# GpSimd makes the lower part of every second half block of split weights

## The chip, the cores and the metric

The kernel runs on one core of one Trainium2 chip. The metric is the device time of one execution in microseconds (us). Before the change three runs took 1807.63 us in the median, from 1806.89 to 1811.34.

## What is computed

The reference passes a 256 x 1024 activation through three blocks, all in float32: a block of chunkwise retention and a gated linear recurrence, a block of windowed attention, convolution and pooling with a convolutional feed-forward network, and a block of two layers, each of a SwiGLU network, a mixer (an RWKV-7 time mix in the first layer, a chunked gMLP in the second), cross-attention to a memory, and a second SwiGLU network.

```python
def reference(x, ...):
    x = first_block(x, ...)    # q,k,v,g,x_lru,g_lru = split(norm(x) @ w_in); retention, RG-LRU; h + mixed @ w_out
    x = second_block(x, ...)   # h = x @ w_in; attention, conv, pool; layer norms; (u * silu(g)) @ w_down
    return third_block(x, ...) # per layer: ffn1, mixer, cross-attention, ffn2, each x + f(rms_norm(x)) @ w
```

Nearly all of the work is products of the 256 rows with weight matrices of 1024 to 5632 columns. Every weight is used once.

## The kernel before, in words

All weights lie in device memory as blocks of 128 x 2048 floats (`WB = 2048`), in the order in which they are used (the plan). For accuracy a product is made from three matmuls: a float32 weight w is split into an upper part hi (w rounded to the matmul's type `fp32r`) and a lower part lo = w - hi; the activations are split likewise, and the product is hi·hi + hi·lo + lo·hi (`mul`, lines 533 to 547, and `mul_tok`, lines 549 to 567; line 547, 563 and 566 are those that read a block's lower part). Only the blocks of three matrices (`WHOLE`: rw_k, rw_v, rw_o) are used unsplit. Each of the four SwiGLU networks takes 33 blocks (22 + 11).

A block goes through these steps, each into one of 21 slots of on-chip memory (SBUF):

- `_dma` (line 429): SyncE (SP) issues the load of one raw block into a free slot.
- `_split` (line 444): makes half a block. It takes a slot for hi and lo of this half, issues the copy that rounds hi on ScalarE (ACT, line 455), and leaves the subtraction that makes lo on VectorE (DVE, line 458) in `self.rest`. The subtraction is issued by the next call of `_rest`. After that of the second half (`part` is 1) the raw block's slot is given back.
- `pump` (line 478): called after every eight or so groups of matmuls. It issues loads while there are slots to spare, then one `_split`, up to `SPLIT = 4` blocks ahead of the block in use, and else `_rest`.
- `take` and `second` (lines 498 and 518): hand a block to the matmuls. `_need` (line 509) first makes whatever half is not yet made.

There is no scheduler behind this: each engine executes its instructions in the order in which the program issues them. VectorE's queue holds, beside the 524 subtractions of line 458, nearly all elementwise work of the mixers, the norms and the evictions from the matmul's accumulators (PSUM). GpSimd (POOL) has 33 small instructions: memsets, eight copies of four columns (line 1819, `pend`), and one masking of the gMLP's 128 x 2048 mixing weights (`affine_select`, line 1557).

Of the kernel before, what the change touches and what calls it, by code (L numbers as in the profile page):

```python
# [10 lines left out]
F32 = mybir.dt.float32  # L11
# [290 lines left out]
class Net:  # L302
# [138 lines left out]
        self.queue = max(self.queue, self.clock + self.LAT) + us  # L441
        return self.queue

    def _split(self):

        i, part = self.split_i, self.part
        t = self.slot([P, 2, WB // 2], R32)
        if part == 0:
            self.hl[i] = Block()
        self.hl[i].parts.append(t)  # L450
        s = slice(part * WB // 2, (part + 1) * WB // 2)
        hi, lo = t[:, 0], t[:, 1]
        raw = self.raw[i]
        self._rest()
        self.nc.scalar.copy(hi, raw[:, s])  # L455

        def rest():
            self.nc.vector.tensor_sub(lo, raw[:, s], hi.bitcast(F32))  # L458
            if part:
                self.drop(self.raw.pop(i))  # L460
        self.rest, self.rest_of = rest, (i, part)
        self.part = 1 - part
        self.split_i += part

    def _whole(self):

# [42 lines left out]
    def _need(self, i, part):  # L509
        while (self.split_i, self.part) <= (i, part):  # L510
            if self.dma_i <= i:
                self._dma()
            if not self._whole():
                self._split()
        if self.rest and self.rest_of <= (i, 1):
            self._rest()

# [1773 lines left out]
```

## Time and profile before

| what | value |
|---|---|
| median of three runs | 1807.63 us |
| the profiled execution, its own time | 1807.12 us |
| its span (first to last instruction) | 1805.4 us |
| TensorE matmul busy (PE) | 1776.4 us |
| VectorE busy (DVE) | 1256.9 us |
| ScalarE busy (ACT) | 914.0 us |
| GpSimd busy (POOL) | 13.4 us |

The time around the span is 1.7 us. PE is the matmul engine, PEld its weight loads, which overlap the matmuls. A busy share is an average over stages with different limits; what a stage is bound by is read from the windows, the waits and the chain of that stage. Names such as s, t, psd and psx are the program's tiles: s and t lie in SBUF, psd and psx in PSUM. L458 is line 458.

### The profile page before, as it was taken

How to read it: one execution, taken by the hardware profiler on the slowest of the kernel's cores; microseconds unless marked ns; L12 is line 12 of the kernel's file. 1: busy time of each engine (PE TensorE's matmuls, PEld its weight loads, DVE VectorE, ACT ScalarE, POOL GpSimd, SP SyncE). 2: the span in 40 equal slices, each digit the busy share in tenths (PEclk: the TensorE clock that was granted, in tenths of full speed). 3: DMA queues.
4: the chain of work that ended last, by engine and by line, in shares of the span. 5: the costliest groups of instructions: out<-in, count | busy, mean ns of one | idle time of the engine just before them, and what ended most of it. 6: DMA issues, size and time to landing. Idle time of an engine off the chain costs nothing.

```text
span 1805.4 us, 27651 instructions
## 1 busy us (share of the span) xinstructions
PE 1776.4 (98%) x11142; PEld 1552.9 (86%) x11142; DVE 1256.9 (70%) x2300; ACT 914.0 (51%) x1550; POOL 13.4 (1%) x33
## 2 busy tenths in 40 slices
PE   9999999999999999999999999999999999999997
PEld 8899889899887888888698888888888899888886
DVE  7897878997757646678777765566556588675553
ACT  7778455665536544072225554444444455454451
POOL 0000000000000000001000000000000000000000
PEclk9999999999999999999899999999999999999999
DMA  8445435454553645603433454455445636345450
GB/s 317 148 184 207 172 140 214 163 186 162 210 210 140 210 163 187 238 24 117 141 118 118 186 187 163 169 216 198 164 163 190 254 117 229 145 169 182 163 187 24
DMA packets 55495, 310.34 MB, mean 172 GB/s; under 512 B 13727, under 2 KB 16840, under 8 KB 19144
## 3 DMA queue, kind: packets, MB, share of 16 engines
q1 hardware_dynamic: 55368, 308.59, 47.0%
q8 instruction: 87, 1.43, 0.3%
q14 instruction: 40, 0.33, 0.1%
HBM read 304.36 MB, written 4.21 MB: 171 GB/s over the span
## 4 chain that ended last, share of the span: by engine, by line
PE 89%; DVE 7%; ACT 2%; issue 1%; DMA 1%; SPq 0%; DVEq 0%; ACTq 0%
PE psd L543 17%; PE psd L547 14%; PE psd L562 10%; PE psd L564 10%; PE psd L563 10%; PE psd L545 5%; PE psd L546 5%; DVE s L458 2%; PE psx L543 2%; PE psd L2169 2%; PE psd L557 1%; PE psd L540 1%; PE psx L1451 1%; PE psx L547 1%; ACT s L366 1%
## 5 line engine op out<-in xcount | busy, mean ns | idle before, releaser
L458 DVE TENSOR_TENSOR s<-s,s 128x1024 fp32r<-128x1024 f32 x524 | 627.1, 1221 | 169.8 <-ACT s L455 169.4
L547 PE MATMUL psd<-s,s 128*128 128x256 f32 x2336 | 656.8, 281 | 3.0 <-DVE s L458 2.8
L455 ACT CAST s<-s 128x1024 fp32r<-128x1024 f32 x524 | 532.2, 1046 | 179.9 <-PE psd L547 99.8
L543 PE MATMUL psd<-s,s 128*128 128x512 f32 x1392 | 492.7, 398 | 0.9 <-DVE s L629 0.9
L547 PEld LDWEIGHTS psd<-s,s 128*128 128x128 f32 x2336 | 443.1, 190 | 4.7 <-DVE s L458 4.2
L562 PE MATMUL psd<-s,s 128*128 128x512 f32 x816 | 323.8, 397 | 0.7 <-ACT s L366 0.7
L564 PE MATMUL psd<-s,s 128*128 128x512 f32 x816 | 318.6, 390 | 0.7 <-DVE s L369 0.7
L563 PE MATMUL psd<-s,s 128*128 128x512 f32 x816 | 317.8, 389 | 0.0
L543 PEld LDWEIGHTS psd<-s,s 128*128 128x128 f32 x1392 | 261.4, 188 | 64.0 <-DVE s L629 1.3
L545 PE MATMUL psd<-s,s 128*128 128x256 f32 x944 | 271.7, 288 | 0.0
L546 PE MATMUL psd<-s,s 128*128 128x256 f32 x944 | 266.9, 283 | 0.0
L564 PEld LDWEIGHTS psd<-s,s 128*128 128x128 f32 x816 | 153.1, 188 | 34.1 <-DVE s L369 1.3
L545 PEld LDWEIGHTS psd<-s,s 128*128 128x128 f32 x944 | 180.8, 192 | 1.6 <-DVE s L458 0.6
L546 PEld LDWEIGHTS psd<-s,s 128*128 128x128 f32 x944 | 180.9, 192 | 0.1
L562 PEld LDWEIGHTS psd<-s,s 128*128 128x128 f32 x816 | 153.3, 188 | 31.6 <-ACT s L366 1.0
L563 PEld LDWEIGHTS psd<-s,s 128*128 128x128 f32 x816 | 153.4, 188 | 30.5
L1455 DVE TENSOR_TENSOR s<-psx,s 128x512 fp32r<-128x512 f32 x44 | 30.4, 692 | 94.7 <-ACT s L1457 79.2
L366 ACT ACTIVATE t<-psd,rc 128x256 f32<-128x256 f32 x88 | 41.5, 475 | 99.1 <-PE psd L564 96.5
L1457 ACT CAST s<-psx 128x512 fp32r<-128x512 f32 x40 | 23.5, 587 | 120.7 <-PE psx L1451 120.7
L369 DVE SCALAR_TENSOR_TENSOR t<-psd,rc,t 128x256 f32<-128x256 f32 x88 | 41.5, 482 | 47.5 <-ACT t L366 47.5
L366 ACT ACTIVATE t<-x 128x256 f32<-128x256 f32 x86 | 34.2, 407 | 69.1 <-DVE x L369 45.2
L366 ACT ACTIVATE s<-x,vecs 128x256 fp32r<-128x256 f32 (+1 forms) x80 | 40.2, 505 | 49.5 <-DVE x L1415 36.3
(382 smaller groups left out, 1848.8 us busy)
## 6 DMA issues: line engine op xcount, KB each, us to landing
s<-w_ffn_in SPq DMA_DIRECT2D x88, 1024.0 KB, 4.8
s<-w_ffn_out SPq DMA_DIRECT2D x44, 1024.0 KB, 4.8
s<-w_up SPq DMA_DIRECT2D x22, 1024.0 KB, 4.8
s<-w_out SPq DMA_DIRECT2D x12, 1024.0 KB, 5.0
s<-w_down SPq DMA_DIRECT2D x11, 1024.0 KB, 4.8
s<-w_xq SPq DMA_DIRECT2D x8, 1024.0 KB, 5.8
s<-w_xo SPq DMA_DIRECT2D x8, 1024.0 KB, 5.2
s<-w_gm_v SPq DMA_DIRECT2D x8, 1024.0 KB, 4.8
```

What stands on the lines that cost most here:

```text
L366: return self.nc.scalar.activation(out, in_, func, **kw)
L369: return self.nc.vector.scalar_tensor_tensor(out, in0, scalar, in1, op0=op0, op1=op1)
L455: self.nc.scalar.copy(hi, raw[:, s])
L458: self.nc.vector.tensor_sub(lo, raw[:, s], hi.bitcast(F32))
L543: mm(out, w[0], x.two(k), start=first, stop=False)
L545: mm(out[:, :T], w[0], x.hi(k), start=first, stop=False)
L546: mm(out[:, :T], w[0], x.lo(k), start=False, stop=False)
L547: mm(out[:, :T], w[1], x.hi(k), start=False, stop=last)
L562: mm(out, hi, w[0], start=first, stop=False)
L563: mm(out, hi, w[1], start=False, stop=False)
L564: mm(out, lo, w[0], start=False, stop=last)
L2169: mm(ps[:, :P], blocks[m // 2][j * P:(j + 1) * P][0], yo[:, k, o], start=k == 0, stop=k == KD - 1)
```

## The change

The subtraction of every second half of a block is issued to GpSimd instead of VectorE, directly behind the copy on ScalarE and not at the next `_rest`, and the raw block's slot is given back there. First halves stay on VectorE. A second half that `_need` makes because the matmuls want it at once (`now=True`) stays on VectorE as before.

```diff
-    def _split(self):
+    def _split(self, now=False):
         i, part = self.split_i, self.part
         t = self.slot([P, 2, WB // 2], R32)
...
         self._rest()
         self.nc.scalar.copy(hi, raw[:, s])
+        self.part = 1 - part
+        self.split_i += part
+        if part and not now:
+            self.nc.gpsimd.tensor_sub(lo, raw[:, s], hi.bitcast(F32))
+            self.drop(self.raw.pop(i))
+            return
 
         def rest():
             self.nc.vector.tensor_sub(lo, raw[:, s], hi.bitcast(F32))
             if part:
                 self.drop(self.raw.pop(i))
         self.rest, self.rest_of = rest, (i, part)
-        self.part = 1 - part
-        self.split_i += part
...
             if not self._whole():
-                self._split()
+                self._split(now=True)
```

## Rows read from the trace of the kernel before

**Rows 1.** The page's first part: busy us, share of the span, instructions.

```profile
PE 1776.4 (98%) x11142; PEld 1552.9 (86%) x11142; DVE 1256.9 (70%) x2300; ACT 914.0 (51%) x1550; POOL 13.4 (1%) x33
```

**Rows 2.** Waits: who waited for whom, us in total, times, longest.

```profile
PE psd L547 <- DVE s L458: 2.8, 4, 1.6
...
PE psx L1089 <- DVE acc L1079: 0.8, 1, 0.8
...
PE psd L543 <- DVE s L629: 0.9, 1, 0.9
...
SPq L434 <- DVE s L458: 489.0, 85, 23.2
```

**Rows 3.** Groups by line: busy us, mean ns | idle before, releaser.

```profile
L458 DVE TENSOR_TENSOR s<-s,s 128x1024 fp32r<-128x1024 f32 x524 | 627.1, 1221 | 169.8 <-ACT s L455 169.4
```

**Rows 4.** Timeline, GpSimd's copies beside VectorE: start, us, engine, what.

```profile
806.64 1.02 POOL L1819 COPY pend<-e 128x4 f32<-128x4 f32 x1
...
812.69 0.19 POOL L1819 COPY pend<-e 128x4 f32<-128x4 f32 x1 [0.42 <-ACT e L366]
...
806.40 1.22 DVE L458 TENSOR_TENSOR s<-s,s 128x1024 fp32r<-128x1024 f32 x1
```

**Rows 5.** Timeline, VectorE beside GpSimd's masking, and the same operation elsewhere.

```profile
1406.44 2.01 POOL L1557 TENSOR_SCALAR_AFFINE_SELECT s<-s 128x2048 f32<-128x2048 f32 x1 [554.24 <-DMA s<-ws]
...
1406.80 1.67 DVE L374 TENSOR_SCALAR rc<-rcv 128x2 int32<-128x2 int32 x1
...
559.72 0.17 DVE L374 TENSOR_SCALAR rc<-rcv 128x2 int32<-128x2 int32 x1
```

**Rows 6.** Windows: length, busy us (count) of PE, PEld, DVE, ACT, POOL; clock, DMA, GB/s.

```profile
25.00:50.00 25.00, 24.88 (x143) 22.11 (x144) 24.40 (x48) 20.42 (x38) 0.00 (x0) 1.00 0.70 272
...
75.00:100.00 25.00, 24.78 (x201) 23.80 (x201) 24.14 (x46) 18.09 (x30) 0.00 (x0) 1.00 0.44 152
100.00:125.00 25.00, 25.00 (x203) 24.60 (x202) 24.66 (x54) 15.85 (x38) 0.00 (x0) 1.00 0.44 165
...
1100.00:1125.00 25.00, 25.00 (x117) 20.75 (x116) 13.61 (x16) 12.27 (x16) 0.00 (x0) 1.00 0.44 160
...
1450.00:1475.00 25.00, 23.36 (x197) 23.16 (x196) 23.83 (x40) 14.59 (x24) 0.00 (x0) 1.00 0.36 127
```

**Rows 7.** Groups by line on VectorE between 25 and 50 us.

```profile
L369 DVE SCALAR_TENSOR_TENSOR s<-s,vecs,s 128x253 f32<-128x253 f32 (+2 forms) x24 | 11.3, 481 | 0.6
L458 DVE TENSOR_TENSOR s<-s,s 128x1024 fp32r<-128x1024 f32 x7 | 8.4, 1218 | 0.0
```

**Rows 8.** The same between 75 and 125 us.

```profile
L458 DVE TENSOR_TENSOR s<-s,s 128x1024 fp32r<-128x1024 f32 x17 | 20.4, 1217 | 0.5 <-ACT s L455 0.5
```

**Rows 9.** The same between 350 and 400 us.

```profile
L458 DVE TENSOR_TENSOR s<-s,s 128x1024 fp32r<-128x1024 f32 x22 | 26.7, 1218 | 1.6 <-ACT s L455 1.6
L369 DVE SCALAR_TENSOR_TENSOR t<-psd,vecs,t 128x255 f32<-128x255 f32 (+1 forms) x38 | 18.1, 479 | 0.7
```

**Rows 10.** The same between 1450 and 1475 us.

```profile
L458 DVE TENSOR_TENSOR s<-s,s 128x1024 fp32r<-128x1024 f32 x11 | 13.2, 1216 | 0.0
```

**Rows 11.** The chain that ended last, 300 to 335 us: start, us, what.

```profile
316.46 2.35 DVE s L458 x2
...
325.09 3.49 DVE s L458 x3
```

**Rows 12.** Timeline of ScalarE's copies at four tight places, and one subtraction.

```profile
20.87 1.03 ACT L455 CAST s<-s 128x1024 fp32r<-128x1024 f32 x1
...
63.46 1.03 ACT L455 CAST s<-s 128x1024 fp32r<-128x1024 f32 x1
...
64.53 1.23 DVE L458 TENSOR_TENSOR s<-s,s 128x1024 fp32r<-128x1024 f32 x1 [1.87 <-ACT s L455]
...
555.05 3.88 ACT L455 CAST s<-s 128x1024 fp32r<-128x1024 f32 x4
...
1447.34 1.98 ACT L455 CAST s<-s 128x1024 fp32r<-128x1024 f32 x2
```

## The prediction, as it was put on record before the result was known

> **What bounds the kernel now.** I read the page's engine line first. TensorE is busy 1776.4 us of the span of 1805.4 [rows 1], so all that any change off TensorE can give back is 1805.4 - 1776.4 = 29.0 us, the start and the end of the program among them. VectorE at 1256.9 us is not the bound on average. The waits come next: TensorE waited for a subtraction of line 458 four times, 2.8 us together and 1.6 the longest, and about 0.8 or 0.9 us for each of two other VectorE results [rows 2]. So nearly everywhere the split weights lie ready before they are wanted. The windows say where that is less sure: in a long feed-forward stage VectorE is busy 13.61 of 25 us with TensorE at 25.00, but in the first block it is busy 24.40, 24.14 and 24.66 of 25, and in the gMLP 23.83 [rows 6]. There VectorE has no time left, and whatever it loses it can't make up in that stage.
>
> **What is removed.** 524 subtractions at 1221 ns [rows 3], half of them second halves: 262. With four waits on line 458 in all [rows 2] few can be urgent ones, so I count 262 moved. On VectorE each costs 1.17 us, since two in a row take 2.35 [rows 11]: 262 x 1.17 = 307 us less on an engine that is not the bound. This by itself is worth only what TensorE waits for.
>
> **What is added.** 262 two-input operations of 128 x 1024 on GpSimd. The trace has none. The nearest row is the masking, 2048 elements read once in 2.01 us [rows 5]. From below: 1024 elements at that rate, 1.0 us, if both inputs come at once. From above I allow 4.0 us, twice that row. I take 2.0 us: two inputs of 1024 are as many elements read as in that row. 262 x 2.0 = 524 us on GpSimd, which has 13.4 us of other work [rows 1], so GpSimd itself has room.
>
> By the Trainium skill (GPSIMD Engine Reference, Performance versus the Vector engine) an addition of 2048 float32 elements takes GpSimd 4497 ns, two inputs sharing one read port. Half of that would be an estimate of 2.25 us; the sum below would grow by 3.9 us. No run here shows it yet.
>
> **The two engines exclude each other.** This is what the price hangs on. A GpSimd copy of four columns takes 0.19 us at 812.69, but 1.02 us at 806.64, and then it ends at 807.66, just as the VectorE subtraction that began at 806.40 and took 1.22 us ends [rows 4]. The other way round, a VectorE operation on two columns, 0.17 us at 559.72, took 1.67 us at 1406.80 and ended at 1408.47, with the masking on GpSimd that ran from 1406.44 to 1408.45 [rows 5]. So each 2.0 us on GpSimd may close VectorE for 2.0 us to instructions that read two tiles in SBUF (s<-s,s), while 1.17 us are saved: a loss of up to 0.83 us of VectorE time for each half moved. Instructions that read PSUM and one SBUF tile (t<-psd,vecs,t) I take to go on.
>
> The Trainium skill says the same of such instructions (SBUF — State Buffer, Who interferes with whom): an exclusive lock, one side waits for the whole of the other's instruction. The two pairs of rows agree; that it holds for a two-input VectorE operation behind a GpSimd subtraction no row here shows.
>
> **The sum, stage by stage.** Where VectorE has slack (13.61 of 25 us [rows 6]) the exchange costs nothing: the first lower parts are wanted long after they are made. That cover would go only if GpSimd took about 4 us (a rival below). In the full stages:
> - 25 to 50 us: 7 subtractions [rows 7], 3.5 moved: -3.5 x 1.17 = -4.1. Blocked: 3.5 x 2.0 x the share of two-tile instructions in what stays. Line 369 there is s<-s,vecs,s, 11.3 us, and with half of line 458's 8.4 that is 15.5 of the 20.2 left, 0.77; other small groups have the same form, so I take 0.9: +6.3. Net +2.2, of which the 0.6 us of idle time [rows 6] takes some: 1.6 us late. TensorE waits for line 458 in this part, so I count it whole.
> - 75 to 125 us: 17 subtractions [rows 8], 8.5 moved: -9.9; blocked at the same share 8.5 x 2.0 x 0.9 = +15.3; idle 0.86 + 0.34 [rows 6]: 4.2 us late. TensorE is at 24.78 and 25.00, so the weights are some way ahead; I count half, 2.1.
> - 350 to 400 us: 22 subtractions [rows 9], 11 moved: -12.9. Line 369 there reads PSUM, 18.1 us that are not blocked, beside 13.4 us of line 458 that stays; with small groups the blocked share is about 0.54: +11.9. Nothing.
> - 1450 to 1475 us: 11 subtractions [rows 10], 5.5 moved: -6.4; share about 0.8: +8.8; idle 1.2 [rows 6]: +1.2.
> Then single places, where a second half falls into a chain that TensorE waits for. The copy that began at 20.87 ends at 21.9, GpSimd holds until 23.9 and a chain of tiny VectorE operations (a reciprocal root) stands still: 2.0 less the 1.17 saved, +0.8. The copy of 63.46 ends at 64.5; the lower part is ready at 66.5 and not at 65.76 (64.53 + 1.23): +0.7. At 555.05 four copies in a row give GpSimd two subtractions ahead of another such chain: +0.8. At 1447.34 two copies, the first one a second half: GpSimd runs from about 1448.3 to 1450.3, over the chain that ends in the wait of 1.6 us for line 458: +2.0 [rows 2, 12].
> Gains: between 300 and 335 us VectorE is the chain, with pairs of subtractions (2.35) and a run of three (3.49) [rows 11]. Half of them leave, and TensorE's two waits there, 0.8 (L1089) and 0.9 (L629) [rows 2], go: -1.7. What is late next is TensorE itself, whose matmuls stand in a fixed order, so the 4 us and more that VectorE gains there give no more.
> Sum: 1.6 + 2.1 + 0 + 1.2 + 0.8 + 0.7 + 0.8 + 2.0 - 1.7 = +7.5 us.
>
> **Moved steps.** The raw block's slot is given back one pump earlier, so SP is told of the next load earlier, but it then waits for GpSimd instead of VectorE. SP waits for line 458 now, 489.0 us in 85 waits up to 23.2 [rows 2], and TensorE doesn't notice; lower parts that end up to 0.83 us later, or some us earlier where they stood behind other VectorE work, change nothing. It costs something only where weights are scarce, which are the stages counted above. Behind a waiting GpSimd subtraction stand GpSimd's own 33 instructions, most of them memsets far from any split; the eight copies of line 1819 lie in a stage with four split blocks, and I cost them at nothing (one late by 2.0 us would cost at most that).
>
> The profiled execution took 1807.12 us: 1807.1 + 7.5 = 1814.6. The median of the runs lies 0.5 above it: **1815.1 us**.
>
> **The rivals.**
> *Faster: VectorE's relief reaches TensorE.* The second halves no longer stand in VectorE's queue in front of evictions and norms, and GpSimd begins right behind the copy. It needs the short subtraction: below 1.17 us GpSimd blocks VectorE for less than it saves, so that is the point from which it decides. For it speaks that VectorE is the chain from 300 to 335 us [rows 11]; against it the two pairs of rows on exclusion. The three waits of rows 2 make 4.5 us; with as much again hidden in delayed evictions, a quarter of the 29.0 us: -7, 1800.6.
> *No change.* GpSimd falls into VectorE's gaps, the losses of single places are 0.8 here and there and the gains 1.7; it also is the result if most halves turn out urgent and stay on VectorE, so that the change doesn't do what it says. For it: TensorE at 25.00 in most windows. 1807 to 1809.
> *Far slower: GpSimd takes 4 us.* In the feed-forward window TensorE runs 117 matmuls [rows 6], 24 a block (four steps, two halves of the rows, three matmuls): 4.9 blocks, one in 5.1 us. GpSimd would close 4.9 x 4.0 = 19.6 us, and of VectorE's 13.61 us 13.61 - 4.9 x 1.17 = 7.9 stay: 27.5 us do not fit into 25, 10% too much. The four SwiGLU networks have 132 blocks, 670 us; since part of the 7.9 us reads PSUM I take half of 10%: +34, 1841. It decides from about (25 - 7.9) / 4.9 = 3.5 us.
>
> **How the numbers follow.** A change within 0.3%, 5.4 us, is what a measurement of this kernel can't tell from none. The forecast (slower, 1813.1 to 1823, its own range, the upper end from 2.25 us a subtraction and the 75 to 125 us term counted whole) has 0.41; far slower 0.07; no change 0.30; faster 0.22. So slower 0.48, same 0.30, faster 0.22. The range holds 8 in 10 from 1800 (most of the faster case) to 1836 (about 2.7 us a subtraction in the full stages); the far end of the last rival is left out.
>
> **What would show it.** Right: GpSimd has about 262 subtractions; VectorE operations of 0.17 or 0.42 us that last 1 to 2 us beside them; TensorE waits for VectorE that grow before 130 us and near 1450 us; feed-forward windows unchanged at 25.00. Wrong: two-tile VectorE operations of ordinary length beside a GpSimd subtraction (then the exclusion is not there and the faster rival stands), a subtraction far from 2.0 us, or a loss that sits in stages where VectorE had slack.

## The result, and the profile after

The changed kernel takes 1832.53 us in the median (1830.45 to 1833.55), the kernel before 1808.97 in the same comparison: ratio 1.0126, 95% interval 1.0113 to 1.0139. Slower was forecast, and 1832.5 lies inside the range, but the forecast loss was 7.5 us and the measured one 23.6.

The page of the changed kernel, its first part and the two groups that the subtraction of lower parts has become (line 460 on GpSimd, 465 on VectorE):

```profile
PE 1785.3 (98%) x11142; PEld 1559.7 (85%) x11142; DVE 1173.5 (64%) x2038; ACT 912.9 (50%) x1550; POOL 686.8 (38%) x295
...
L460 POOL TENSOR_TENSOR s<-s,s 128x1024 fp32r<-128x1024 f32 x262 | 674.4, 2579 | 1070.9 <-ACT s L456 993.1
...
L465 DVE TENSOR_TENSOR s<-s,s 128x1024 fp32r<-128x1024 f32 x262 | 399.0, 1524 | 206.6 <-ACT s L456 205.3
```

All 262 second halves moved, so the change does what it says. The profiled span is 1830.7 us against 1805.4. Of the 25.3 us more, TensorE is busy 8.9 us longer with the same 11142 matmuls (1785.3 against 1776.4 [rows 1]), and idle 16.4 us longer (45.4 against 29.0). These are two different losses: the matmuls themselves became slower somewhere, and TensorE waited more. The subtractions that stayed on VectorE take 1524 ns on average where they took 1221 [rows 3].

The waits of TensorE for results of other engines, the largest of the whole run (the matmul's line, then the line of the result):

```profile
PE psx L873 <- DVE t L374: 5.1, 1, 5.1
PE psd L550 <- DVE s L965: 4.1, 3, 2.5
...
PE psx L1001 <- DVE e L993: 3.7, 1, 3.7
PE psd L552 <- DVE s L465: 2.1, 3, 0.8
PE psx L1456 <- DVE t L369: 1.8, 2, 1.6
PE psx L1590 <- DVE s L373: 1.5, 2, 1.3
...
PE psd L552 <- POOL s L460: 1.1, 1, 1.1
```

The first three are new, all on VectorE, and all before 150 us. Only 1.1 us is a wait for GpSimd itself. The windows there (columns as in [rows 6]), a calm one, and the gMLP:

```profile
25.00:50.00 25.00, 20.31 (x117) 18.34 (x117) 22.50 (x40) 15.54 (x27) 7.92 (x4) 0.93 0.66 260
...
75.00:100.00 25.00, 23.66 (x188) 22.34 (x187) 23.66 (x35) 12.76 (x22) 9.92 (x4) 1.00 0.36 126
100.00:125.00 25.00, 21.23 (x158) 20.52 (x156) 23.53 (x31) 14.38 (x24) 9.87 (x4) 0.93 0.58 211
125.00:150.00 25.00, 20.93 (x149) 20.52 (x150) 22.14 (x43) 16.23 (x47) 7.46 (x3) 0.86 0.32 127
...
1100.00:1125.00 25.00, 25.00 (x116) 20.69 (x115) 8.22 (x10) 10.64 (x14) 12.00 (x5) 1.00 0.51 182
...
1475.00:1500.00 25.00, 23.49 (x183) 23.10 (x182) 23.58 (x27) 11.33 (x18) 12.26 (x5) 0.93 0.33 123
```

In the first block VectorE is nearly as full as before, TensorE has lost about 4 us in some windows, and the granted clock has fallen to 0.86. In the calm window VectorE went from 13.61 us to 8.22 and TensorE stayed at 25.00.

How one loss comes about, in the timeline of the changed kernel: GpSimd's subtractions, and the chain of two-column operations on VectorE that ends in the matmul of line 873.

```profile
22.63 2.38 POOL L460 TENSOR_TENSOR s<-s,s 128x1024 fp32r<-128x1024 f32 x1 [5.12 <-ACT s L456]
25.95 2.34 POOL L460 TENSOR_TENSOR s<-s,s 128x1024 fp32r<-128x1024 f32 x1 [0.94 <-ACT s L456]
```

```profile
22.65 2.38 DVE L676 TENSOR_TENSOR sa<-rc 128x2 f32<-128x2 f32 x1
25.06 0.16 DVE L369 SCALAR_TENSOR_TENSOR sa<-sa,sv 128x2 f32<-128x2 f32 x1
...
26.04 2.26 DVE L369 SCALAR_TENSOR_TENSOR rc<-sa,rc 128x2 f32<-128x2 f32 x1
28.33 0.48 DVE L374 TENSOR_SCALAR t<-misc,rc 128x128 f32<-128x128 f32 x2
```

An operation on two columns that takes 0.16 us takes 2.38, from just behind the start of GpSimd's subtraction to its end, and six operations later another one 2.26. TensorE's 5.1 us wait is for what follows, the row at 28.33. (The second TensorE loss, the clock, is read further down.)

### The profile page after: what moved, and what is told of

Its sections match the earlier page's. It is cut to its first block, busy times and chain, and to the rows that moved or that the text cites. A ratio compares the mean times of both kernels' runs of the same rounds, so it can differ in the third digit from the quotient of the medians.

```text
span 1830.7 us, 28055 instructions
## 1 busy us (share of the span) xinstructions
PE 1785.3 (98%) x11142; PEld 1559.7 (85%) x11142; DVE 1173.5 (64%) x2038; ACT 912.9 (50%) x1550; POOL 686.8 (38%) x295
## 4 chain that ended last, share of the span: by engine, by line
PE 78%; DVE 11%; ACT 2%; issue 1%; DMA 1%; DVEq 0%; SPq 0%; ACTq 0%
PE psd L548 17%; PE psd L552 12%; PE psd L567 9%; PE psd L569 9%; PE psd L568 9%; PE psd L550 4%; PE psd L551 4%; DVE s L465 2%; PE psx L548 2%; PE psd L2174 1%; DVE t L369 1%; PE psx L1456 1%; PE psx L552 1%; ACT s L456 1%; PE psx L1496 1%
## 5 line engine op out<-in xcount | busy, mean ns | idle before, releaser
L460 POOL TENSOR_TENSOR s<-s,s 128x1024 fp32r<-128x1024 f32 x262 | 674.4, 2579 | 1070.9 <-ACT s L456 993.1
L465 DVE TENSOR_TENSOR s<-s,s 128x1024 fp32r<-128x1024 f32 x262 | 399.0, 1524 | 206.6 <-ACT s L456 205.3
```

Of the source, the lines that this page charges most:

```text
L460: self.nc.gpsimd.tensor_sub(lo, raw[:, s], hi.bitcast(F32))
```

## The experiments

The theory going in: while GpSimd reads, VectorE's two-tile operations stand still; this hurts where VectorE is full, in the first block above all. Against it stood the changed order (the subtraction issued earlier, the slot given back earlier), lower parts that merely come later from GpSimd, and a loss spread over the program. All edits are to the changed kernel.

**Everywhere but the first 24 blocks, and there alone.**

```diff
-        if part and not now:
+        if part and not now and i >= 24:
```

> GpSimd makes the second lower parts of all blocks but the first 24 (those of the first network's input products, in use until about 140 us); these stay on VectorE. Theory (exclusion hurts where VectorE is full, 22 of the 24 us are lost in this part): about 1813, ratio to before 1.002 (the later stages lose 4 to 5 us net). Rival 'order' (the earlier hand-out of slots and of the subtraction shifts the whole program): the loss is spread, about 1822 or more. Rival 'a late start is made up later': with the first part undisturbed the later stages lose more than they did, above 1818.

```diff
-        if part and not now:
+        if part and not now and i < 24:
```

> The complement: GpSimd makes the second lower parts of the first 24 blocks alone, all others as before. Theory: 1809 + 22 = 1831, ratio 1.012, with the delay against before complete by 140 us and TensorE at half clock for two or three stretches there. Rival 'spread over the program': 1813 or less.

Measured: 1810.99 us without the first 24 blocks, ratio to before 1.0011 (1.0002 to 1.0020); 1830.51 with them alone, 1.0118 (1.0102 to 1.0134). Nearly the whole loss, 21 us, belongs to the 23 halves that move in these blocks, and the other 239 together cost about 1.5 us (0.4 to 3.6 by the interval). TensorE's waits before 150 us in the first of the two runs:

```profile
PE psx L779 <- DVE t L776: 1.3, 1, 1.3
...
PE psx L873 <- DVE t L374: 1.0, 1, 1.0
```

The 5.1 at line 873 has become 1.0, and the 4.1 and 3.7 are gone.

**The order alone.**

```diff
-            self.nc.gpsimd.tensor_sub(lo, raw[:, s], hi.bitcast(F32))
+            self.nc.vector.tensor_sub(lo, raw[:, s], hi.bitcast(F32))
```

> The changed order alone: the second lower parts are issued directly behind the copy, and the raw slot is given back there, but on VectorE. Theory (the engine costs the time, not the order): within 5 us of before, 1804 to 1814. Rival 'order' (subtractions put in front of evictions in VectorE's queue, other slots): 1825 to 1833, as the changed kernel.

1812.03 us, ratio 1.0008 (0.9998 to 1.0017), so at most about 3 us. The order is not the cause of the 23.6. It may have a small part in the first block, where TensorE in this trace waits 1.6 us at line 1001, as it doesn't in the kernel before; but the next two versions have the same order and are faster than the kernel before.

**GpSimd writes but doesn't read.**

```diff
-            self.nc.gpsimd.tensor_sub(lo, raw[:, s], hi.bitcast(F32))
+            self.nc.gpsimd.memset(hi[:, :1].bitcast(F32), 0.0)
+            for _ in range(2):
+                self.nc.gpsimd.memset(lo.bitcast(F32), 0.0)
```

> In place of each subtraction GpSimd fills one column of the upper part (so that it waits for the copy as the subtraction does) and writes the lower part twice with zeros: it writes but reads nothing. This leaves the second lower parts out. GpSimd is busy about as long (0.1 + 2 x 0.96 = 2.0 us against 2.4). Theory (it is GpSimd's reading that closes VectorE's two-tile operations): VectorE operations of ordinary length beside it, and the time at or below that of before, 1800 to 1810. Rival 'late lower parts' (they come from GpSimd later than from VectorE, exclusion or not): above 1822.

1800.08 us, ratio 0.9943 (0.9931 to 0.9956). Its groups on GpSimd and VectorE (line 462 is the memset, 467 the subtraction that stayed), and the chain of two-column operations beside one pair of memsets:

```profile
L462 POOL MEMSET s<- 128x1024 f32 x524 | 500.2, 956 | 15.1
...
L467 DVE TENSOR_TENSOR s<-s,s 128x1024 fp32r<-128x1024 f32 x262 | 320.2, 1223 | 207.0 <-ACT s L456 206.8
```

```profile
23.44 1.97 POOL L462 MEMSET s<- 128x1024 f32 x2
...
23.59 0.16 DVE L369 SCALAR_TENSOR_TENSOR sa<-sa,sv 128x2 f32<-128x2 f32 x1
```

GpSimd is busy 500 us beside VectorE, VectorE's subtractions take 1223 ns, as before, and the two-column operation its 0.16 us. So neither GpSimd's being busy nor a lower part that is ready 2.0 us behind the copy costs anything; what costs is a GpSimd instruction that reads. This version also shows about what the move would be worth without the exclusion: 9 us.

**GpSimd reads one input.**

```diff
-            self.nc.gpsimd.tensor_sub(lo, raw[:, s], hi.bitcast(F32))
+            self.nc.gpsimd.memset(hi[:, :1].bitcast(F32), 0.0)
+            self.nc.gpsimd.tensor_copy(lo, raw[:, s])
```

> In place of each subtraction GpSimd fills one column of the upper part (to wait for the copy) and then copies the raw half to the lower part: one input read, about 1.0 us. This leaves the subtraction out. Theory (the loss goes with the time for which GpSimd reads; below the 1.17 us that VectorE saves it turns into a gain): VectorE stalls of up to 1.0 us beside it, and 1800 to 1811, between the write-only kernel and before. Rival 'any reading GpSimd instruction costs a fixed handover': 1818 or more.

1802.09 us, ratio 0.9961 (0.9948 to 0.9974). The copy, VectorE's remaining subtraction, and one place where a copy meets the chain of two-column operations:

```profile
L461 POOL CAST s<-s 128x1024 fp32r<-128x1024 f32 x262 | 293.3, 1120 | 0.3 <-issue 0.3
```

```profile
L466 DVE TENSOR_TENSOR s<-s,s 128x1024 fp32r<-128x1024 f32 x262 | 325.8, 1244 | 212.1 <-ACT s L456 211.2 <-issue 0.8
```

```profile
23.04 1.04 POOL L461 CAST s<-s 128x1024 fp32r<-128x1024 f32 x1
...
23.17 0.92 DVE L369 SCALAR_TENSOR_TENSOR sa<-sa,sv 128x2 f32<-128x2 f32 x1
```

It reads, but for 1.12 us on average and not 2.4, about what VectorE saves, and the sign of the change turns. The two-column operation is held to the end of the copy, 0.92 us, so a single input excludes VectorE too, for as long as it is read. That it is the length alone and not the number of inputs that decides the time isn't shown: no one-input operation of 2.4 us was run.

**Two instructions of half the length.**

```diff
-            self.nc.gpsimd.tensor_sub(lo, raw[:, s], hi.bitcast(F32))
+            for c in range(2):
+                q, o = slice(c * 512, c * 512 + 512), part * WB // 2 + c * 512
+                self.nc.gpsimd.tensor_sub(t[:, 1, q], raw[:, o:o + 512], t[:, 0, q].bitcast(F32))
```

> Each GpSimd subtraction issued as two of 512 columns. Theory (the exclusion lasts as long as one instruction): the longest stalls of tiny VectorE operations beside GpSimd fall from 2.2 us to 1.2 us and more of them are hit; the time stays within 6 us of the changed kernel's, 1826 to 1836, since in the full stages a two-tile operation is always waiting. Rival 'not by instruction': stalls of 2.2 us stay, or none changes.

1830.76 us, ratio 1.0120 (1.0107 to 1.0133). The same chain in this run:

```profile
22.86 1.31 DVE L373 TENSOR_SCALAR softplus<-softplus 128x8 f32<-128x8 f32 x2
24.09 1.24 DVE L374 TENSOR_SCALAR sv<-sv 128x2 f32<-128x2 f32 x1
...
26.55 1.16 DVE L369 SCALAR_TENSOR_TENSOR sa<-sa 128x2 f32<-128x2 f32 x1
27.75 1.19 DVE L369 SCALAR_TENSOR_TENSOR rc<-sa,rc 128x2 f32<-128x2 f32 x1
```

Four stalls of about 1.2 us in place of two of 2.3 (the first row merges two operations that take 0.24 us together when nothing holds them): one side waits for one whole instruction of the other, then gets its turn. The sum, and the time, stay.

**The place at 22 to 28 us.**

```diff
-        if part and not now:
+        if part and not now and i not in (2, 3):
```

> The changed kernel with blocks 2 and 3 back on VectorE, whose GpSimd subtractions lay over the chain of tiny operations at 22 to 28 us. Theory (that place costs its wait of 5.1 us, and the stretch at half clock after it): 5 to 7 us less than the changed kernel, about 1826. Rival 'the backlog costs the same a little later': 1830 or more.

1829.67 us, ratio 1.0114 (1.0101 to 1.0127). By the ratios to before this is 2.2 us less than the changed kernel, but the two intervals overlap; the time lies next to the rival's 1830 and not at the theory's 1826. TensorE's waits in the first 60 us, and a window:

```profile
PE psx L912 <- DVE s L369: 1.8, 2, 1.4
...
PE psx L873 <- DVE t L374: 1.2, 1, 1.2
```

```profile
25.00:50.00 25.00, 22.09 (x127) 18.74 (x128) 24.40 (x44) 17.73 (x33) 5.00 (x2) 1.00 0.65 259
```

The 5.1 became 1.2, a gain of 3.9, and the stretch at the lower clock is gone here (1.00 against 0.93). But VectorE is full behind it, and the wait of line 912 grew from 1.2 to 1.8. Matched matmul by matmul, the profiled execution is 3.9 us ahead of the changed kernel's behind the chain and only 2.1 us ahead at 114 us: part of a stall that is removed comes back later while the engine that caused it has a backlog.

**The middle alone, and the calm stretches too.**

```diff
-        if part and not now:
+        if part and not now and 32 <= i <= 85:
```

> GpSimd makes the second lower parts of blocks 32 to 85 alone (from the second network's input product to the start of the first SwiGLU, about 200 to 550 us), where in e1_rest_only TensorE gained 3.7 us against before; all other blocks as before. Theory (a trade between the exclusion and a shorter queue on VectorE, decided by each stage): 1805.8, ratio 0.998, with the wait for L629 after 320 us gone. Rival 'GpSimd never pays, the gain was the order of the slots or chance': 1809.5 or more.

```diff
-        if part and not now:
+        if part and not now and (32 <= i <= 85 or 92 <= i <= 119 or 147 <= i <= 212 or 250 <= i):
```

> GpSimd makes the second lower parts of blocks 32 to 85 as in e5_middle_only, and of blocks 92 to 119, 147 to 212 and from 250 on, which lie in the calm stretches of the four SwiGLU networks and behind them: 173 more. Theory (where VectorE has slack the exclusion costs nothing): as e5_middle_only, ratio to before 0.998, about 1806.5. Rival 'every moved half costs a little' (0.83 us of VectorE each, of which TensorE would pay a tenth: 14 us): 1815 or more.

1806.35 us, ratio 0.9983 (0.9973 to 0.9994), and 1806.64 us, 0.9986 (0.9974 to 0.9998). (The second moves 173 halves in all, 119 more than the first; the expectation misnamed the sum.) Both are ahead of the kernel before by about 0.15%, with intervals that end just below 1. With the middle alone TensorE waits for no other engine between 300 and 340 us, line 629 included. The first windows are those of the kernel before from 300 to 350 us, the second those of the version with the middle alone:

```profile
300.00:325.00 25.00, 24.22 (x137) 20.83 (x136) 22.19 (x43) 7.30 (x13) 0.00 (x0) 1.00 0.62 243
325.00:350.00 25.00, 23.84 (x169) 21.89 (x169) 21.95 (x42) 16.61 (x33) 0.00 (x0) 1.00 0.22 80
```

```profile
300.00:325.00 25.00, 25.00 (x144) 21.69 (x143) 20.68 (x38) 7.29 (x14) 10.32 (x5) 1.00 0.66 245
325.00:350.00 25.00, 24.73 (x179) 23.21 (x178) 20.66 (x40) 17.72 (x36) 8.34 (x3) 1.00 0.22 77
```

TensorE gains 0.78 + 0.89 = 1.7 us there. In the run with the order alone the same two windows have 24.21 and 24.28 us of matmuls, so most of the gain belongs to GpSimd and not to the order. The 119 halves in calm stretches add and take nothing that can be measured.

## Why the prediction was right in its way and too small in its size

- **The number.** 1832.5 lies in the range, but by luck: none of the cases that the prediction priced ends there (1813.1 to 1823 for the forecast itself), and the range reached to 1836 for another reason, about 2.7 us a subtraction in the full stages.
- **The mechanism** was right. GpSimd's reading and VectorE's two-tile operations exclude each other, instruction by instruction (and some of one tile too, last section). It shows in the stall of 2.38 us, and by its absence where GpSimd only writes. The Trainium skill's rule (SBUF — State Buffer, Who interferes with whom), which holds it for instructions with two SBUF inputs against GpSimd instructions that read and not against those that only write, agrees with 1524 ns against 1223 here. That instructions with one input in PSUM go on was taken rightly too: between 75 and 125 us of the changed kernel those of line 965 keep their length, while those of line 968 with two SBUF inputs are held.

```profile
L968 DVE TENSOR_TENSOR t<-t,s 128x256 f32<-128x256 f32 x11 | 8.3, 752 | 0.0
...
L965 DVE TENSOR_TENSOR s<-psd,s 128x256 f32<-128x256 f32 x12 | 5.0, 419 | 0.8 <-ACT t L964 0.8
```

  The point from which it decides, a hold of 1.17 us, lies between the runs: 1.12 gains, 2.4 loses, and nothing in between was run. The faster rival's 1800.6 is near the 1802.09 of the one-input copy, but by luck, since its 7 us were a guessed quarter of 29.0.
- **The subtraction on GpSimd** was taken at 2.0 us; undisturbed it takes about 2.34 to 2.38 (the mean of 2579 ns has GpSimd's own waits for VectorE in it). The reading "as many elements as the masking reads" left out that two inputs cost more than their sum, 2 x 1.04 us by the copy above. The Trainium skill's figure (GPSIMD Engine Reference, Performance versus the Vector engine) gave an estimate of 2.25, nearer. By the prediction's own scale (3.9 us for 0.25) the 0.38 us more are worth 5.9 us.
- **The first block** is the step that failed: forecast 1.6 + 2.1 + 0.8 + 0.7 = 5.2 us, measured 21. In the profiled executions, matched matmul by matmul, the delay is 22.3 us by the end of this part: 15.9 us of it are idle time of TensorE, most of the rest is the clock (below). The term of 75 to 125 us was halved because "the weights are some way ahead". That is no cover here, since the long waits are not for weights. TensorE waits for line 965, which empties a PSUM accumulator and stands in VectorE's queue behind operations that GpSimd holds, and for line 993:

```profile
109.14 2.42 POOL L460 TENSOR_TENSOR s<-s,s 128x1024 fp32r<-128x1024 f32 x1 [3.74 <-ACT s L456]
```

```profile
109.23 2.88 DVE L944 TENSOR_TENSOR_SCAN s<-s,s 128x256 f32<-128x256 f32 x1
...
112.80 0.42 DVE L965 TENSOR_TENSOR s<-psd,s 128x256 f32<-128x256 f32 x1
```

  The scan of line 944 takes 0.68 us when nothing holds it; the wait of 2.5 us for line 965 ends with the last row. Counted whole and at 2.4 us the term is 8.5 x (2.4 x 0.9 - 1.17) - 1.2 = 7.2, and TensorE's waits for lines 965 and 993 are 4.1 + 3.7 = 7.8. Its waits for lower parts (line 552, above) are 2.1 + 1.1 us in the whole run. The place at 20.87 us was counted as one hit, 0.8 us; two subtractions hit the same chain, and the wait is 5.1 us. The place at 64 us was 1.1 us and not 0.7.
- **Later stages** were forecast at 0 + 1.2 + 0.8 + 2.0 - 1.7 = +2.3 us, measured +1.5 without the first 24 blocks. The sum is near, its terms are not all. The gain of 1.7 between 300 and 335 us came as worked out. Of the 2.0 us at 1447 no longer wait came: TensorE's 1.6 us for line 458 [rows 2] have become 1.5 us at line 1590 for line 373. The place at 555 us was too small at 0.8: GpSimd does hold the chain there (2.18 us for an operation of 0.17), TensorE waits 1.6 us at line 1456 behind it, and one of the stretches at the lower clock lies there.
- **The clock** was missing from the sum. Five stretches of the changed kernel:

```profile
28.80:32.20 3.40, 3.33 (x13) 3.15 (x14) 2.05 (x7) 1.15 (x3) 0.00 (x0) 0.50 1.02 424
114.10:117.50 3.40, 3.40 (x19) 3.40 (x18) 3.37 (x5) 0.00 (x0) 1.08 (x1) 0.50 1.01 419
131.20:138.00 6.80, 5.15 (x24) 5.15 (x25) 6.66 (x17) 4.52 (x11) 0.19 (x1) 0.50 0.00 0
...
578.30:581.70 3.40, 3.40 (x10) 2.63 (x9) 2.73 (x3) 1.65 (x2) 3.40 (x2) 0.51 0.00 0
1479.40:1482.80 3.40, 3.40 (x18) 3.40 (x17) 2.63 (x6) 2.90 (x5) 0.12 (x1) 0.51 0.02 5
```

  The granted clock is 0.50, the lower of its two levels, for 13.6 us in the first three and 20.4 in all; at half speed that is up to 10.2 us of matmul time. The kernel before has none of the five: 25 to 175 us are at 1.00 throughout, as in this window,

```profile
125.00:150.00 25.00, 25.00 (x209) 24.83 (x208) 19.79 (x50) 23.20 (x78) 0.00 (x0) 1.00 0.52 183
```

  and its two low stretches later on (3.4 us at 780, 10.2 us at 892) have their like in the changed kernel (at 821 and 916). So the clock can account for the 8.9 us by which TensorE is busier. The first three follow waits: 5.1 us at line 873, those for line 965, 3.7 us at line 1001. But not each such wait is followed by one. In the version with the first 24 blocks alone TensorE waits 3.7 us for line 965 between 100 and 125 us, and the window stays at 1.00:

```profile
100.00:125.00 25.00, 21.28 (x171) 20.68 (x171) 23.49 (x34) 15.23 (x26) 9.23 (x4) 1.00 0.58 211
```

  Without the waits the low stretches before 150 us are gone (everywhere but the first 24 blocks) or fewer (6.8 us of them in place of 13.6, without blocks 2 and 3). That the clock falls because of the waits is likely by this, and what decides when it does stays open.
- **Calm stages** cost nothing, as said: 1100 to 1125 us at 25.00, and the timed version with 119 more halves there. **The moved steps** were costed at nothing, and the order alone has ratio 1.0008. **GpSimd at 4 us** did not occur.

## What to carry to other kernels

Before work goes to an idle engine, ask what it shares with the busy one, and look for a pair of rows in which both run: a two-column operation that takes ten times its time is enough to see it. Price such a move by what the receiving engine's instruction blocks, against what the giving engine saves, and do so stage by stage: the same move lost 21 us in the first block, where the giving engine was full, cost nothing where it had slack, and gained where it was the chain. Where waits are added to the engine that sets the time, leave room in the sum and the range for its clock. And ask what each wait is for: that one operand lies ready is no cover for a result that stands in the same queue.

## What the runs showed that was not expected

- VectorE as a whole was relieved even so: it is busy 1173.5 us against 1256.9 before. Against the write-only version's 969.8 us the stalls make 203.7 us, 0.78 us for each half moved, less than the 1.17 saved. The average said gain; the stage said loss.
- Two GpSimd subtractions of 512 columns take 2 x 1450 ns on average where one of 1024 takes 2579, with the waits in it.
- Not only operations with two input tiles stand still. In the version with half the length, `TENSOR_SCALAR` operations with one input tile are held as well (the rows of 1.31 and 1.24 us, above). The second of them in the changed kernel, before GpSimd starts at 22.63:

```profile
22.25 0.16 DVE L374 TENSOR_SCALAR sv<-sv 128x2 f32<-128x2 f32 x1
```

  So the prediction's "two-tile" was too narrow for the small operations; the operation of its own second pair, `rc<-rcv` [rows 5], has one input tile as well. The Trainium skill (SBUF — State Buffer, Who interferes with whom) says that `tensor_scalar` can take the shared ports; this pair of rows agrees.
